# Nine warm-up products instead of fourteen ahead of a two-layer hybrid decoder trunk

## The chip, the cores and the metric
The kernel runs on one core of a Trainium2 chip. The metric is the time of one execution in device microseconds (us), the median of three runs. A NeuronCore has five engines that run side by side and wait for each other by semaphores: PE (TensorE, matrix products), DVE (VectorE), ACT (ScalarE), POOL (GpSimd) and SP (SyncE, which here issues the DMAs). Each engine takes its own instructions strictly in the order in which they stand in the program.

## What is computed
One sequence of 256 tokens with 1024 channels goes through two layers. Each layer normalizes its input, multiplies it by one large input projection, and feeds two groups of heads: attention (8 heads of 128, which for 256 tokens is plain causal attention with a linear distance bias, since no past block exists) and a Mamba-2 state space group (16 heads of 64). Both are gated, joined, and multiplied by an output projection.

```python
def hybrid_layer(x, ln_w, w_in, ...):
    h = rms_norm(x, ln_w)
    proj = h @ w_in
    q, k, v, g_attn, z, xbc, dt_raw = jnp.split(proj, cuts, axis=-1)
    q = rms_norm(q...); k = rms_norm(k...)
    attn = moba_attention(q, k, v) * jax.nn.silu(g_attn)
    xbc = jax.nn.silu(causal_depthwise_conv(xbc, conv_w, conv_b))
    dt = jax.nn.softplus(dt_raw + dt_bias)
    y = ssd_scan(xs, bm, cm, dt, a_log, d_skip) * jax.nn.silu(z)
    y = rms_norm(y, ssd_norm_w)
    return x + jnp.concatenate([attn, y], axis=-1) @ w_out
```

The warm-up products of this study are no part of that: they multiply a tile of ones by itself into a PSUM tile that nobody reads.

## The kernel before
**Weights.** All projections are done in three products, so that float32 accuracy survives a faster product format: with an operand split into a rounded part and a rest, high x high, low x high and high x low are summed in PSUM (lines 226 to 228 for token-major outputs, 244 to 246 for channel-major ones). The weights come in steps of two 128-row slices. Step number i is loaded by SP into `raw` i (line 79), ACT rounds it to `wh` i (line 101), DVE subtracts to get the rest, `wl` i (line 102). There are four `raw` buffers, so the load of `raw` i+4 waits until `wl` i has been computed, and eight pairs of `wh` and `wl`. PE then spends twelve products on a step, the first few of which need only `wh`. Steps 0 to 11 are the value projection v (chunks of 348, 348 and 344 columns), 12 to 27 are q and k, 28 to 39 are the convolved channels x (products `xb`), then the gates g and z, and the output projection.

**The first layer's start.** The transposed input `xT` arrives by DMA and is scaled by the norm's weight without the norm's own factor (`hr`, `lr`, lines 297 and 298), so that the v products can start before the norm is known; the factor is applied to v when it leaves PSUM. Meanwhile ACT sums the squares of the input, POOL takes the power (line 185), DVE puts the factors on a diagonal (`dg`, line 316), PE spreads them over all rows by a product with ones (`rg`, line 321), and DVE multiplies all eight slices of `xT` by them (line 325), which ACT and DVE split into `hT` and `lT` for q, k, x, g and z.

**The warm-up.** Before the first v product, line 165 issues WARM products of a 128 x 128 tile of ones with itself, in plain float32, which the hardware takes as two passes each. They wait for nothing but the memset of the ones (line 159).

**What sets the order.** The kernel is written as a stream of projection steps, between which side work (norms, attention heads, scans) is resumed a given number of steps later (`resume` and `tick`). Yet the order in the program is not that of the source. Except in two regions put under a manual schedule (the first loads and splits on ACT, DVE and SP; the last PE stretch of a layer), the framework orders each engine's instructions by a timeline that it reckons when the kernel is built. What the kernel issues at its start therefore also moves what that timeline puts first later on. Once built, the order is fixed.

**The decay.** From dt_raw, DVE computes a short chain (lines 399 to 412), PE sums it along the sequence (`cp`, line 415), DVE copies it (`cT`, line 418), SP writes it to DRAM (`cd`, line 420) and reads it back twice, broadcast to all 128 partitions, 1 MB each (`cb`, line 423). ACT and DVE make the decay matrices from `cb` (`ehi`, line 470; lines 471 to 474).

**Attention.** After q and k have been normalized (squares `qsq` on ACT, line 342) and transposed (`qtp`, line 354), a head's scores `sp` (lines 362 and 363) are turned into probabilities `sc` by DVE and ACT (lines 365 to 376), transposed by PE (`pp`, line 380) and multiplied by v (`po`, lines 386 and 387).

Of the kernel before, what the change touches and what calls it, by code (L numbers as in the profile page):

```python
# [113 lines left out]


RAWB = 4
WARM = 14
URGENT = 400


# [1 line left out]
def hybrid_kernel(ctx: ExitStack, tc: tile.TileContext, x, par, w, out):  # L122
# [40 lines left out]

    for i in range(WARM):
        pe.matmul(warm[:, 0:P], ones, ones, start=(i == 0), stop=(i == WARM - 1))

# [602 lines left out]
```

## Time and profile before

| | |
|---|---|
| median of three runs | 452.83 us (452.31 to 452.98) |
| the profiled execution's own time | 452.3 us |
| its span, first to last instruction | 450.5 us |
| PE busy | 446.1 us, 99% of the span |
| DVE, ACT, POOL busy | 346.7, 279.7, 23.9 us |
| warm-up products | 28 passes, from 1.05 to 7.02 us |

The span is 1.8 us shorter than the execution's time. A line of the time-ordered view reads: start in us, duration in us, engine, source line, operation, tile written and tiles read, shapes, how many instructions are merged into the line, and in brackets the idle time of the engine ahead of it and what ended it. Matrix products overlap in the pipe, so the distance between two starts, and not the duration, tells what one costs. An engine name that ends in q is its instruction queue; SPq lines are DMA issues. Tile names come without their buffer numbers.

### The profile page before, as it was taken

Reading aid. Unit: us, or ns where it says so; the run is one execution under the profiler, and the core shown is the slowest. Engines: PE = TensorE matmul, PEld = TensorE weight load, DVE = VectorE, ACT = ScalarE, POOL = GpSimd, SP = SyncE. Lnnn points to the kernel's source line nnn. Section 1 sums busy time; section 2 is a strip of 40 time slices with the busy share of each in tenths; the row PEclk is TensorE's granted clock in tenths of the full one; section 3 lists DMA queues with packets and bytes.
Section 4 is the critical chain, followed back from the end, with each engine's and each line's share of the span. In section 5 each row is a group of like instructions: output and inputs, shape, how many; then the busy total and the mean of one; then the engine's idle time right before and its main releaser. Section 6 shows DMA issues by size and latency. Waiting matters only on the chain.

```text
span 450.5 us, 7880 instructions
## 1 busy us (share of the span) xinstructions
PE 446.1 (99%) x2956; PEld 406.0 (90%) x2956; DVE 346.7 (77%) x636; ACT 279.7 (62%) x571; POOL 23.9 (5%) x29
## 2 busy tenths in 40 slices
PE   9999999999999999999999999999999999999997
PEld 9998878999999999888899878889999989998986
DVE  7597876799999888766565784686999999787621
ACT  7776779778558645534556656977657865555400
POOL 0000320200000000000000011110000000000000
PEclk9999999999999999999999999999999999999999
DMA  8888886452355155556246988561435444553301
GB/s 282 275 250 294 284 302 249 143 185 95 95 188 176 60 160 186 169 188 182 61 138 232 284 278 288 185 227 53 139 109 175 139 141 128 200 180 121 121 25 70
DMA packets 26373, 79.43 MB, mean 176 GB/s; under 512 B 2624, under 2 KB 9440, under 8 KB 25824
## 3 DMA queue, kind: packets, MB, share of 16 engines
q1 hardware_dynamic: 26048, 78.68, 53.3%
q8 instruction: 23, 0.38, 0.3%
q10 hardware_dynamic: 288, 0.27, 0.2%
q14 instruction: 14, 0.11, 0.1%
HBM read 77.85 MB, written 1.08 MB: 175 GB/s over the span
## 4 chain that ended last, share of the span: by engine, by line
PE 99%; DVE 0%; issue 0%
PE o L227 6%; PE o L226 6%; PE o L228 6%; PE xb L244 5%; PE xb L246 5%; PE xb L245 5%; PE z L245 3%; PE v L228 3%; PE z L244 3%; PE v L226 3%; PE v L227 3%; PE z L246 3%; PE k L227 3%; PE g L246 3%; PE g L244 3%; PE g L245 3%
## 5 line engine op out<-in xcount | busy, mean ns | idle before, releaser
L102 DVE TENSOR_TENSOR wl<-raw,wh 128x1024 fp32r<-128x1024 f32 (+3 forms) x145 | 166.0, 1157 | 41.3 <-ACT wh L101 40.1
L101 ACT CAST wh<-raw 128x1024 fp32r<-128x1024 f32 (+3 forms) x145 | 143.9, 999 | 59.8 <-DMA raw<-in_w_dram 15.9
L244 PE MATMUL xb<-hT,wh 128*128 128x256 f32 x192 | 56.3, 293 | 0.0
L245 PE MATMUL xb<-lT,wh 128*128 128x256 f32 x192 | 54.4, 283 | 0.0
L246 PE MATMUL xb<-hT,wl 128*128 128x256 f32 x192 | 53.9, 281 | 0.0
L245 PEld LDWEIGHTS xb<-lT,wh 128*128 128x128 f32 x192 | 36.2, 189 | 0.3
L246 PEld LDWEIGHTS xb<-hT,wl 128*128 128x128 f32 x192 | 36.2, 189 | 0.1
L244 PEld LDWEIGHTS xb<-hT,wh 128*128 128x128 f32 x192 | 36.2, 188 | 0.2
L246 PE MATMUL g<-hT,wl 128*128 128x256 f32 x128 | 36.3, 283 | 0.0
L245 PE MATMUL z<-lT,wh 128*128 128x256 f32 x128 | 36.2, 283 | 0.0
L244 PE MATMUL g<-hT,wh 128*128 128x256 f32 x128 | 36.1, 282 | 0.0
L244 PE MATMUL z<-hT,wh 128*128 128x256 f32 x128 | 36.0, 281 | 0.0
L245 PE MATMUL g<-lT,wh 128*128 128x256 f32 x128 | 35.9, 281 | 0.0
L246 PE MATMUL z<-hT,wl 128*128 128x256 f32 x128 | 35.9, 280 | 0.0
L447 DVE SCALAR_TENSOR_TENSOR cv<-rw,par_sb,cv 128x256 f32<-128x256 f32 x72 | 31.6, 481 | 4.2 <-ACT cv L444 4.2
L226 PE MATMUL k<-wh,hT 128*128 128x512 f32 x64 | 25.4, 397 | 0.0
L227 PE MATMUL k<-wh,lT 128*128 128x512 f32 x64 | 25.4, 397 | 0.0
L228 PE MATMUL k<-wl,hT 128*128 128x512 f32 x64 | 25.4, 397 | 0.0
L227 PE MATMUL q<-wh,lT 128*128 128x512 f32 x64 | 25.1, 394 | 0.0
L226 PE MATMUL q<-wh,hT 128*128 128x512 f32 x64 | 25.1, 394 | 0.0
L227 PE MATMUL o<-wh,al 128*128 128x512 f32 (+1 forms) x64 | 24.7, 386 | 0.0
L228 PE MATMUL q<-wl,hT 128*128 128x512 f32 x64 | 24.6, 395 | 0.0
(197 smaller groups left out, 1106.6 us busy)
## 6 DMA issues: line engine op xcount, KB each, us to landing
raw<-in_w_dram SPq DMA_DIRECT2D x120, 512.0 KB, 4.3
raw<-in_w_dram SPq DMA_DIRECT2D x15, 348.0 KB, 3.7
cb<-cd SPq DMA_DIRECT2D x4, 1024.0 KB, 7.8
raw<-in_w_dram SPq DMA_DIRECT2D x8, 344.0 KB, 3.6
x<-in_x_dram SPq DMA_DIRECT2D x2, 512.0 KB, 5.2
xT<-in_w_dram SPq DMA_DIRECT2D x3, 256.0 KB, 4.3
out_dram<-x SPq DMA_DIRECT2D x3, 256.0 KB, 2.0
raw<-in_w_dram SPq DMA_DIRECT2D x2, 174.0 KB, 3.2
```

The costliest lines, as they stand in the source:

```text
L101: nc.scalar.copy(h[:, ks, :wd], src[:, ks, :wd])
L102: nc.vector.tensor_tensor(lo[:, ks, :wd], src[:, ks, :wd], h[:, ks, :wd].bitcast(F32), ALU.subtract)
L226: pe.matmul(ps[:, cs], lh[:, kl, tl], wh[:, kk, cs], start=first, stop=False)
L227: pe.matmul(ps[:, cs], ll[:, kl, tl], wh[:, kk, cs], start=False, stop=False)
L228: pe.matmul(ps[:, cs], lh[:, kl, tl], wl[:, kk, cs], start=False, stop=final)
L244: pe.matmul(o, wh[:, kk, cs], lh[:, k, :], start=(k == 0 and c == 0), stop=False)
L245: pe.matmul(o, wh[:, kk, cs], ll[:, k, :], start=False, stop=False)
L246: pe.matmul(o, wl[:, kk, cs], lh[:, k, :], start=False, stop=(k == KT - 1 and c == 1))
L447: dve.scalar_tensor_tensor(cv[:, c, :], rw[:, c, k:k + S], cw(k), cv[:, c, :], ALU.mult, ALU.add)
```

## The change
The constant WARM goes from 14 to 9. Line 165 then issues nine warm-up products, 18 passes. Nothing else in the source changes.

```diff
 RAWB = 4
-WARM = 14
+WARM = 9
 URGENT = 400
```

The built program changes beyond that, since the framework's ordering comes out otherwise: on PE, DVE, ACT and SP the order differs in the first layer, from step 6 to step 39; all that follows, the whole second layer included, stands in the same order as before.

The first place is on DVE, from the factors of the first norm (`dg0`) on. `wl8` is the low part that v step 8 needs, and the xT rows are the eight multiplications by the spread factors `rg0`. Before:

```order
L316 TENSOR_SCALAR dg0_302<-ident_124,rs0_185 128x128
L102 TENSOR_TENSOR wl7_233<-raw7_212,wh7_232 128x2x348
L102 TENSOR_TENSOR wl8_251<-raw8_218,wh8_250 128x2x344
L325 SCALAR_TENSOR_TENSOR xT_87<-xl_88,rg0_363 128x256
L325 SCALAR_TENSOR_TENSOR xT_87<-xT_87,xl_88,rg0_363 128x256 x5
L102 TENSOR_TENSOR wl9_269<-raw9_224,wh9_268 128x2x344
```

And in the changed program:

```order
L316 TENSOR_SCALAR dg0_297<-ident_119,rs0_180 128x128
L102 TENSOR_TENSOR wl7_228<-raw7_207,wh7_227 128x2x348
L325 SCALAR_TENSOR_TENSOR xT_87<-xl_88,rg0_358 128x256
L325 SCALAR_TENSOR_TENSOR xT_87<-xT_87,xl_88,rg0_358 128x256 x6
L102 TENSOR_TENSOR wl8_246<-raw8_213,wh8_245 128x2x344
L325 SCALAR_TENSOR_TENSOR xT_87<-xT_87,xl_88,rg0_358 128x256
L102 TENSOR_TENSOR wl9_264<-raw9_219,wh9_263 128x2x344
```

Seven multiplications now stand ahead of `wl8`, where there was none.

The second place is on ACT, around the first work on the broadcast `cb`. Before, the rounding of steps 30 and 31 and the squares of q stood ahead of it:

```order
L101 CAST wh30_790<-raw30_734 128x1024
L342 ACTIVATE qsq_818,ss_819<-q10_732 128x128 x4
L355 ACTIVATE qT0_507<-qtp_695,par_sb_86 128x4x128
L355 ACTIVATE qT0_507<-qtp_701,par_sb_86 128x4x128
L101 CAST wh31_846<-raw31_752 128x1024
L342 ACTIVATE qsq_830,ss_831<-q11_733 128x128 x4
L355 ACTIVATE kT0_508<-qtp_806,par_sb_86 128x4x128
L470 ACTIVATE ehi0_0_1318<-cb0_0_203,nac_209 128x128 x4
```

Now they stand behind its first instructions:

```order
L470 ACTIVATE ehi0_0_1313<-cb0_0_198,nac_204 128x128 x4
L470 ACTIVATE ehi1_0_1451<-cb0_0_198,nac_204 128x128 x2
L101 CAST wh30_785<-raw30_729 128x1024
L470 ACTIVATE ehi1_0_1451<-cb0_0_198,nac_204 128x128 x2
L473 ACTIVATE ehi0_0_1313<-ehi0_0_1313 128x512
L342 ACTIVATE qsq_813,ss_814<-q10_727 128x128 x4
L474 ACTIVATE cb0_0_198<-cb0_0_198 128x1024
L342 ACTIVATE qsq_825,ss_826<-q11_728 128x128
L355 ACTIVATE kT0_503<-qtp_801,par_sb_86 128x4x128
L342 ACTIVATE qsq_825,ss_826<-q11_728 128x128 x3
L355 ACTIVATE kT0_503<-qtp_807,par_sb_86 128x4x128
L101 CAST wh31_841<-raw31_747 128x1024
```

Two castings, eight squares and one transposed k have moved behind the wait for `cb` (the other transposed k already stood behind it). On DVE, `cT` has moved ahead of `wl28`, and on SP the write of `cd` and both reads of `cb` have moved ahead of the loads of `raw32` and `raw33`.

The third place is on PE, at the transposition `pp` of the first head's probabilities. Before, it stood two products into step 29:

```order
L246 MATMUL xb5_1072<-hT0_135,wl28_755 128x256
L244 MATMUL xb5_1072<-hT0_135,wh29_772 128x256
L245 MATMUL xb5_1072<-lT0_136,wh29_772 128x256
L380 MATMUL pp_1039<-ident_124,sc_865 128x128
L354 MATMUL qtp_1045<-ident_124,qn_953 128x128
L380 MATMUL pp_1039<-ident_124,sc_865 128x128 x2
```

Now it stands in the middle of step 28, eight products earlier:

```order
L246 MATMUL xb5_1067<-hT0_130,wl28_750 128x256
L380 MATMUL pp_1034<-ident_119,sc_860 128x128
L354 MATMUL qtp_1040<-ident_119,qn_948 128x128 x2
L380 MATMUL pp_1034<-ident_119,sc_860 128x128 x2
L354 MATMUL qtp_1040<-ident_119,qn_948 128x128 x2
L354 MATMUL qtp_1046<-ident_119,qn_960 128x128 x4
L244 MATMUL xb5_1067<-hT0_130,wh28_749 128x256
```

Around it, what was one stretch of attention products in the row of projection products is now two (the scores `sp` that followed `pp` directly come six products later); the same split happens at two other places, so that there are three more such stretches in all. The `cp` product has moved ahead by fourteen products, to step 20.

## Rows read from the trace of the kernel before
**Rows 1.** Page: busy time of PE; the chain that ended last, by engine
```profile
PE 446.1 (99%) x2956; PEld 406.0 (90%) x2956; DVE 346.7 (77%) x636; ACT 279.7 (62%) x571; POOL 23.9 (5%) x29
...
PE 99%; DVE 0%; issue 0%
```
**Rows 2.** PE in order of time, the start (columns as explained above)
```profile
1.05 5.97 PE L165 MATMUL warm<-ones 128*128 128x128 f32 x28 [1.05 <-DVE ones L159]
...
6.53 0.50 PE L165 MATMUL warm<-ones 128*128 128x128 f32 x3
6.78 0.57 PE L226 MATMUL v<-wh,hr 128*128 128x348 f32 x2
...
20.30 0.61 PE L321 MATMUL rg<-dg,ones 128*128 128x128 f32 x4
```
**Rows 3.** Stretches: length, busy per engine, granted clock, DMA share, GB/s
```profile
1.00:1.50 0.50, 0.45 (x2) 0.45 (x3) 0.12 (x4) 0.00 (x0) 0.39 (x1) 1.00 0.00 0
```
**Rows 4.** ACT and DVE in order of time: operands of steps 0 and 1
```profile
4.34 0.46 ACT L101 CAST wh<-raw 128x348 fp32r<-128x348 f32 x1
...
7.41 0.88 DVE L102 TENSOR_TENSOR wl<-raw,wh 128x696 fp32r<-128x696 f32 x1 [0.31 <-ACT wh L101]
```
**Rows 5.** DVE in order of time, dg, wl8, xT and wl9
```profile
19.20 0.29 DVE L316 TENSOR_SCALAR dg<-ident,rs 128x128 f32<-128x128 f32 x1 [0.68 <-POOL rs L185]
...
21.18 0.88 DVE L102 TENSOR_TENSOR wl<-raw,wh 128x688 fp32r<-128x688 f32 x1 [0.73 <-ACT wh L101]
21.97 0.48 DVE L325 SCALAR_TENSOR_TENSOR xT<-xl,rg 128x256 f32<-128x256 f32 x1
...
24.32 0.87 DVE L102 TENSOR_TENSOR wl<-raw,wh 128x688 fp32r<-128x688 f32 x1
```
**Rows 6.** PE in order of time, where steps 8, 9 and 12 need weights
```profile
23.28 0.32 PE L228 MATMUL v<-wl,hr 128*128 128x344 f32 x1
...
24.99 0.32 PE L227 MATMUL v<-wh,lr 128*128 128x344 f32 x1
25.25 0.43 PE L228 MATMUL v<-wl,hr 128*128 128x344 f32 x1
...
29.08 0.62 PE L226 MATMUL q<-wh,hT 128*128 128x512 f32 x2
```
**Rows 7.** SP's issue of raw12, and ACT's rounding of it
```profile
22.09 0.33 SPq L79 DMA_DIRECT2D raw<-in_w_dram  x1
...
26.89 1.05 ACT L101 CAST wh<-raw 128x1024 fp32r<-128x1024 f32 x1 [0.79 <-DMA raw<-in_w_dram]
```
**Rows 8.** PE in order of time: products after a stretch of attention products
```profile
81.02 0.47 PE L244 MATMUL xb<-hT,wh 128*128 128x256 f32 x1
81.32 0.28 PE L245 MATMUL xb<-lT,wh 128*128 128x256 f32 x1
81.44 0.28 PE L246 MATMUL xb<-hT,wl 128*128 128x256 f32 x1
```
**Rows 9.** DVE, SP, ACT and PE in order of time: from cT to pp
```profile
59.64 0.41 DVE L418 COPY cT<-cp 16x256 f32<-16x256 f32 x1
...
64.43 0.80 SPq L423 DMA_DIRECT2D cb<-cd  x2
...
65.97 1.05 ACT L101 CAST wh<-raw 128x1024 fp32r<-128x1024 f32 x1
66.91 0.29 ACT L342 ACTIVATE qsq<-q 128x128 f32<-128x128 f32 x1
...
67.92 0.72 ACT L355 ACTIVATE kT<-qtp,par_sb 128x512 f32<-128x512 f32 x1
68.66 2.46 ACT L470 ACTIVATE ehi<-cb,nac 128x128 f32<-128x128 f32 x8
...
84.03 0.35 DVE L376 TENSOR_SCALAR sc<-sc,ri 128x256 f32<-128x256 f32 x1
...
86.89 0.27 PE L380 MATMUL pp<-ident,sc 128*128 128x128 f32 x1
```

## The prediction
> **What bounds the kernel now.** The page comes first: PE is busy for 446.1 of 450.5 us, and the chain that ended last lies 99% on PE [rows 1]. So the reader is to look at PE alone, ask where it would wait, and take every delay of PE in the first layer as a delay of the end, since behind it no gap is left in which it could be made up. The time-ordered view of PE's start shows 28 warm-up passes from 1.05 us on and the first real product at 6.78 [rows 2]. The operands of that product are there earlier: its weights are rounded at 4.34 + 0.46 = 4.80 us [rows 4]. The warm-up thus holds real work back by nearly 2 us, and this is what the change can win at most.
>
> The next view is DVE's, further on [rows 5]. At 19.49 us the factors of the first norm are done, then come `wl7`, `wl8` and the xT multiplications. Beside it stands PE's view of steps 8 and 9 [rows 6]: the product at 23.28 is the first that needs `wl8`, and the one at 25.25 the first that needs `wl9`. The eleven products from 23.28 to 24.99 take 0.155 us each, and then the twelfth 0.26. This is the one place in the whole trace where PE waits for a split, and the wait is only 0.1 us long, for `wl9` ends at 24.32 + 0.87 = 25.19. PE and DVE are neck and neck at about 25 us; after that, PE's q and k steps are longer than the splits, and PE alone counts.
>
> **The start.** The first 25 passes take 6.53 - 1.05 = 5.48 us, 0.219 each, the last three 0.25 us, 0.083 each [rows 2]. So PE ran at half pace until about 6.5 us, and at full pace from there on. Eighteen passes end at 1.05 + 18 x 0.219 = 5.0 us, and the first product starts there instead of at 6.78. If the pace rises at 6.5 as before, the first 1.5 us of real products go at half pace (0.32 instead of 0.16 us): 4.7 products. The other 7.3 of step 0 take 1.2 us, to 7.7. In step 1 the fifth product needs `wl1`, which ends at 7.41 + 0.88 = 8.29 [rows 4]: a small wait, then eight products to 9.65. Before, step 2 began 24 products and 0.09 us after 6.78, at 10.71. PE is 1.05 us early there.
>
> [...]
>
> **Where the start's gain ends.** At `rg` PE would arrive 1.05 early, at 19.25. But `rg` needs the second `dg`, done at 19.20 + 0.29 = 19.49 [rows 5], which hangs on the landing of the input and not on PE. So `rg` starts at 19.55, and 0.75 us of the lead are left.
>
> **The reordered DVE queue.** `wl7` follows at about 19.55 as before and holds DVE for 0.79 us (21.18 to 21.97 for its like [rows 5]). `rg` takes 0.61 us and is done at 20.16, so the multiplications start at 20.35, right behind `wl7`. Six of them lie between 21.97 and 24.32, 0.392 each; seven take 2.74 us. `wl8`, which was second in the queue, starts at 23.09 and ends at 23.96. PE comes to the product that needs it at 23.28 - 0.75 = 22.53 and waits until 24.02: 0.74 us later than before. The wait at `wl9` (0.10 us) is gone in exchange. Term one: +0.64 us (bounds 0.4 and 0.9). It does not depend on the start at all, since the chain runs from `dg`.
>
> **The load behind wl8.** The load of step 12 waits for `wl8` to free its buffer. It was issued at 22.09, right behind the end of `wl8` at 22.06, and rounded from 26.89 on, 4.80 us later [rows 7]. From 24.0 this makes 28.8, and `wh12` ends at 29.85; PE wants it at 29.08 + 0.64 = 29.72 [rows 6]. Term two: 0.15 us, between 0 (a quicker landing) and 0.5.
>
> **More switches on PE.** After a stretch of plain float32 attention products, the first projection product takes 0.30 us to the next start instead of 0.12 [rows 8]. Three such stretches are added. At 0.18 us each they would cost 0.54, and after mere transpositions, for which these rows give no price, perhaps nothing. Term three: 0.3 us, between 0 and 0.55.
>
> **The probabilities of the first head.** From the start of `ehi` at 68.66, when the broadcast had landed, to the last multiplication of `sc` (84.03 + 0.35) it takes 15.72 us [rows 9], in which ACT is hardly idle. Into this stretch the new order puts two more roundings (65.97 to 66.91: 0.94 each), eight squares (66.91 to 67.92: 1.01 for four) and one transposed k (0.66): 1.88 + 2.02 + 0.66 = 4.56 us. Against that the broadcast comes earlier, since `cT` no longer stands behind `wl28` and its wait: by 1.1 us (the split alone) to 1.9 (with the wait); I take 1.5, for the weights themselves come somewhat later after term two. So `sc` is ready at 84.38 + 4.56 - 1.5 = 87.45. PE reaches `pp` eight products (0.114 each) ahead of the old place and later by terms one, two and a third of three: 86.89 - 0.91 + 0.64 + 0.15 + 0.1 = 86.87. Term four: 0.6 us of waiting, between 0 (a broadcast 2.1 us early) and 1.7 (0.4 early).
>
> Both reads of `cb` now also stand ahead of two loads. [...] The trace shows the two reads issued together at 64.43, with the first one's consumer starting at 68.66 [rows 9]. [...]
>
> Everything behind step 39, and the second layer, is in the old order, and no wait of PE stands there that could swallow a delay. The sum is 0.64 + 0.15 + 0.3 + 0.6 = +1.7 us. On the profiled execution's own 452.3 us (its span of 450.5 and 1.8 around it) it gives 454.0, and on the median of the runs, which is 0.5 higher, 454.5. I predict **454.2 us**.
>
> **Rivals.** *The lead is kept (faster).* If `wl8` ended before PE comes for it, PE would carry its 0.75 us on and be spared the 0.10 at `wl9`: 452.83 - 0.85 = 452.0. It decides at 22.5 us on DVE: the seven multiplications would have to end 1.5 us earlier than by rows 5. Against it stands that `dg` at 19.49 is unmoved and the order is fixed. Chance 0.07.
>
> *Only the early waits count (about the same).* If the broadcast comes 2 us earlier and the added switches are short, terms four and most of three vanish, and +0.6 to +0.9 remain: 453.5. For it speaks that `cT` has moved past a split and a wait; against it that 4.56 us of work have come between. Chance 0.23.
>
> *The wait at pp is the main cost (slower).* If the broadcast is not early at all and the later loads are held up behind it, `sc` comes 2 us later still: 1.1 + 2.6 = +3.7, 456.5. Chance 0.08.
>
> *The pace rises late (slower).* If it rose at 10 us, 3.5 us more would go at half pace, 1.75 us lost, of which 0.3 is covered by the waits at `wl1` and `dg`: `rg` at 21.0 instead of 19.55, its end at 21.6, the chain behind it 1.2 us later (it had 0.2 to spare), and the wait at `pp` gone: 0.64 + 1.2 + 0.15 + 0.3 = +2.3, 455.1. [...] Chance 0.06.
>
> **How the numbers follow.** The forecast, 453.4 to 455.1, has 0.56. A change under 0.2% (0.9 us) is not told from none by a measurement of this kernel. Faster than that: the first rival, 0.07. Within it: the second, and a little of the forecast's lower end, 0.25. Slower: the rest, 0.68. The range of 452.8 to 455.8 leaves out the first rival, the third and a little of the second.
>
> **What would show it.** In the changed profile: the first v product at 5.0 us; `rg` at about 19.55, right after `dg`; seven xT lines ahead of the `wl` of step 8, PE idle for 1.5 us before the product at about 24.0; q's first product at 29.7 to 30.0; PE waiting for `sc` at `pp`, about 87.4. If `wl8` is done by 22.5, or PE does not wait at `pp` and is not behind there, the prediction is wrong in its main steps; if the first v product goes at half pace beyond 8 us, the clock is.

## The result and the profile after

| | before | nine products |
|---|---|---|
| first measurement, median | 452.82 us (452.31 to 453.45, 10 runs) | 456.75 us (453.59 to 458.00, 10 runs) |
| ratio, with its 95% interval | | 1.0073 (1.0049 to 1.0096) |
| second measurement, with the experiments, median | 452.92 us (451.94 to 453.92, 28 runs) | 454.53 us (453.32 to 456.64, 8 runs) |
| ratio, with its 95% interval | | 1.0036 (1.0019 to 1.0053) |
| profiled execution, its span | 452.3, 450.5 us | 457.47, 455.7 us |

The change makes the kernel slower, as forecast, but by 3.9 us in the first measurement, where 1.4 had been forecast, and 456.75 lies above the range. The second measurement, 454.53, lies inside it. Why two measurements of one program differ by 2.2 us (six of ten runs above 456.3 in the first, one of eight in the second) no run shows; it may be chance. New is the spread: 4.7 us over the 18 runs, against about 2 us over the 38 of before. Eleven of the 18 lie below 455, seven above 456.3, none between. In five of the seven the mean granted clock of the run is 0.995 or 0.996; in all others of the 18 it is 0.998 or more.

The page of the profiled execution shows PE no longer alone on the chain that ended last (before: 99% PE [rows 1]):

```profile
PE 446.0 (98%) x2946; PEld 403.6 (89%) x2946; DVE 346.5 (76%) x636; ACT 279.3 (61%) x571; POOL 24.6 (5%) x29
...
PE 79%; DMA 9%; DVE 4%; ACT 3%; issue 2%; SPq 1%; POOL 0%; ACTq 0%; DVEq 0%; POOLq 0%
```

PE is busy as long as before, 446.0 us against 446.1, and now also waits. The view of waits of the same execution names them (what waits, for whom; us in total, times, longest):

```profile
PE pp L380 <- DVE sc L375: 1.9, 1, 1.9
PE v L226 <- ACT wh L101: 1.5, 2, 1.2
PE v L228 <- DVE wl L102: 1.4, 1, 1.4
PE warm L165 <- DVE ones L159: 1.0, 1, 1.0
PE rg L321 <- DVE dg L316: 0.4, 1, 0.4
```

Take them in order of time. PE starts real work at 4.86 us instead of 6.78 [rows 2]:

```profile
1.05 3.73 PE L165 MATMUL warm<-ones 128*128 128x128 f32 x18 [1.05 <-DVE ones L159]
4.86 0.59 PE L226 MATMUL v<-wh,hr 128*128 128x348 f32 x2
5.29 0.48 PE L227 MATMUL v<-wh,lr 128*128 128x348 f32 x2
5.61 0.48 PE L228 MATMUL v<-wl,hr 128*128 128x348 f32 x2
```

In the trace the first fourteen passes start 0.21 us apart and the last four 0.11 us apart: the full pace is there from about 4.2 us on, more than 2 us earlier than in the trace of before (6.5) and after fewer products. PE then waits 0.3 us for the rounded weights. The lead of 1.9 us does not last. In this execution the load of `raw2`, issued at 3.43 us against 3.44 before, lands 2 us late. The rounding of `raw2` on ACT shows it, first before:

```profile
8.16 0.78 ACT L101 CAST wh<-raw 128x696 fp32r<-128x696 f32 x1
```

and after:

```profile
10.13 0.77 ACT L101 CAST wh<-raw 128x696 fp32r<-128x696 f32 x1 [2.07 <-DMA raw<-in_w_dram]
```

The input lands late as well (ACT starts on its second half at 19.07 us, before at 16.99), and `dg` is done at 21.57 us instead of 19.49 [rows 5]. DVE, after:

```profile
21.28 0.29 DVE L316 TENSOR_SCALAR dg<-ident,rs 128x128 f32<-128x128 f32 x1 [0.68 <-POOL rs L185]
21.64 0.88 DVE L102 TENSOR_TENSOR wl<-raw,wh 128x696 fp32r<-128x696 f32 x1
22.45 0.47 DVE L325 SCALAR_TENSOR_TENSOR xT<-xl,rg 128x256 f32<-128x256 f32 x1
22.84 2.43 DVE L325 SCALAR_TENSOR_TENSOR xT<-xT,xl,rg 128x256 f32<-128x256 f32 x6
25.19 0.87 DVE L102 TENSOR_TENSOR wl<-raw,wh 128x688 fp32r<-128x688 f32 x1
```

`wl8` stands behind seven multiplications, and PE waits 1.36 us for it, where before it had none (23.28 [rows 6]):

```profile
24.43 0.32 PE L227 MATMUL v<-wh,lr 128*128 128x344 f32 x1
26.11 0.42 PE L228 MATMUL v<-wl,hr 128*128 128x344 f32 x1 [1.36 <-DVE wl L102]
...
31.80 0.39 PE L226 MATMUL q<-wh,hT 128*128 128x512 f32 x1
```

The first q product is 2.7 us later than the 29.08 of [rows 6]. The other large wait is at the first head's probabilities. On ACT, after:

```profile
70.44 1.87 ACT L470 ACTIVATE ehi<-cb,nac 128x128 f32<-128x128 f32 x6 [4.84 <-DMA cb<-cd]
72.22 1.04 ACT L101 CAST wh<-raw 128x1024 fp32r<-128x1024 f32 x1
```

and on DVE and PE:

```profile
60.95 0.41 DVE L418 COPY cT<-cp 16x256 f32<-16x256 f32 x1
...
90.95 0.35 DVE L376 TENSOR_SCALAR sc<-sc,ri 128x256 f32<-128x256 f32 x1
```
```profile
88.98 0.28 PE L246 MATMUL xb<-hT,wl 128*128 128x256 f32 x1
91.18 0.30 PE L380 MATMUL pp<-ident,sc 128*128 128x128 f32 x1 [1.92 <-DVE sc L375]
```

ACT idles for 4.84 us in front of `ehi`, waiting for the broadcast `cb`, while the castings and squares that filled that time before [rows 9] are queued behind it. `cT` is ahead in DVE's order, yet 1.3 us later than before (60.95 against 59.64), and `ehi` 1.8 us later (70.44 against 68.66). The sum `cp` that `cT` copies is done on PE at 57.81. But two other splits still stand ahead of `cT`, and ACT rounds their weights late, since it has waited for a load. ACT and DVE, after:

```profile
56.58 1.05 ACT L101 CAST wh<-raw 128x1024 fp32r<-128x1024 f32 x1 [1.78 <-DMA raw<-in_w_dram]
```
```profile
57.66 1.23 DVE L102 TENSOR_TENSOR wl<-raw,wh 128x1024 fp32r<-128x1024 f32 x1 [1.25 <-ACT wh L101]
...
59.74 1.23 DVE L102 TENSOR_TENSOR wl<-raw,wh 128x1024 fp32r<-128x1024 f32 x1 [0.76 <-ACT wh L101]
```

### The profile page after: what moved, and what is told of

The parts are those of the page before. It is cut to its first block, busy times and chain, and to the rows that moved or that the text cites. A ratio compares the mean times of both kernels' runs of the same rounds, so it can differ in the third digit from the quotient of the medians.

```text
span 455.7 us, 7859 instructions
## 1 busy us (share of the span) xinstructions
PE 446.0 (98%) x2946; PEld 403.6 (89%) x2946; DVE 346.5 (76%) x636; ACT 279.3 (61%) x571; POOL 24.6 (5%) x29
## 4 chain that ended last, share of the span: by engine, by line
PE 79%; DMA 9%; DVE 4%; ACT 3%; issue 2%; SPq 1%; POOL 0%; ACTq 0%; DVEq 0%; POOLq 0%
DMA raw<-in_w_dram 7%; PE o L227 6%; PE o L226 6%; PE o L228 6%; PE xb L244 4%; PE xb L246 4%; PE xb L245 4%; PE z L245 3%; PE z L244 3%; PE z L246 3%; PE g L246 3%; PE g L245 3%; PE g L244 3%; PE yp L498 3%; ACT wh L101 2%
## 5 line engine op out<-in xcount | busy, mean ns | idle before, releaser
L244 PE MATMUL xb<-hT,wh 128*128 128x256 f32 x192 | 56.2, 293 | 0.0
L245 PE MATMUL xb<-lT,wh 128*128 128x256 f32 x192 | 54.3, 283 | 0.0
L245 PEld LDWEIGHTS xb<-lT,wh 128*128 128x128 f32 x192 | 36.2, 189 | 0.3
L244 PEld LDWEIGHTS xb<-hT,wh 128*128 128x128 f32 x192 | 36.2, 189 | 0.2
L245 PE MATMUL z<-lT,wh 128*128 128x256 f32 x128 | 36.2, 283 | 0.0
L244 PE MATMUL g<-hT,wh 128*128 128x256 f32 x128 | 36.1, 282 | 0.0
L244 PE MATMUL z<-hT,wh 128*128 128x256 f32 x128 | 36.0, 281 | 0.0
L245 PE MATMUL g<-lT,wh 128*128 128x256 f32 x128 | 35.9, 281 | 0.0
L228 PE MATMUL k<-wl,hT 128*128 128x512 f32 x64 | 25.5, 398 | 0.0
L185 POOL TENSOR_TENSOR rr<-se,mhalf 128x4 f32<-128x4 f32 x16 | 18.8, 1178 | 122.2 <-DVE se L344 122.2
L228 PE MATMUL q<-wl,hT 128*128 128x512 f32 x64 | 24.8, 395 | 0.0
```

The costliest lines, as they stand in the source:

```text
L185: pool.tensor_tensor(o, i, mhalf[:, :n], ALU.pow)
L228: pe.matmul(ps[:, cs], lh[:, kl, tl], wl[:, kk, cs], start=False, stop=final)
L244: pe.matmul(o, wh[:, kk, cs], lh[:, k, :], start=(k == 0 and c == 0), stop=False)
L245: pe.matmul(o, wh[:, kk, cs], ll[:, k, :], start=False, stop=False)
```

## The experiments

The framework's order depends on the number of warm-up products, so the change is two changes: a shorter start, and another order. The experiments cross them. The order can be held: an edge that only orders (no semaphore) from each instruction to its neighbour in a list taken from either built program. Every engine then has the wanted order word for word, whatever WARM says.

| kernel | start | order to step 15 | order behind | median, range (us), runs | ratio to before (95%) | runs with clock 0.996 or less |
|---|---|---|---|---|---|---|
| short_start_old_order | 9 | before | before | 453.21, 452.51 to 453.77, 11 | 1.0007 (0.9999 to 1.0016) | 0 |
| long_start_new_order | 14 | after | after | 454.52, 453.49 to 457.62, 9 | 1.0048 (1.0030 to 1.0066) | 1 |
| after_again | 9 | after | after | 454.53, 453.32 to 456.64, 8 | 1.0036 (1.0019 to 1.0053) | 1 |
| short_start_old_early | 9 | before | after | 454.24, 452.73 to 457.44, 12 | 1.0034 (1.0017 to 1.0051) | 1 |
| short_start_old_late | 9 | after | before | 453.57, 453.21 to 454.14, 11 | 1.0009 (1.0001 to 1.0018) | 0 |
| short_start_old_pe | 9 | after, PE before | after, PE before | 454.86, 454.16 to 456.19, 6 | 1.0044 (1.0029 to 1.0059) | 0 |
| short_start_filled_pp | 9 | after | after | 455.90, 455.28 to 456.97, 6 | 1.0068 (1.0054 to 1.0082) | 0 |
| long_start_late_sc | 14 | before | before, ACT loaded | 457.33, 456.68 to 459.03, 5 | 1.0085 (1.0068 to 1.0101) | 2 |
| short_start_x_early | 9 | before, x earlier | before | 452.51, 451.91 to 453.20, 11 | 0.9991 (0.9982 to 1.0000) | 0 |
| short_start_best | 9 | rearranged | before | 451.43, 451.24 to 452.47, 6 | 0.9965 (0.9951 to 0.9980) | 0 |
| short_start_best_again | 9 | rearranged | before | 451.54, 451.21 to 452.46, 11 | 0.9968 (0.9958 to 0.9979) | 0 |
| long_start_best | 14 | rearranged | before | 451.94, 451.09 to 452.55, 7 | 0.9975 (0.9965 to 0.9986) | 0 |

The kernel before, run beside them 78 times in all, had no run with a granted clock under 0.998. Line numbers in the traces of experiments are higher by the lines put in (L244 or L245 is L228, L396 and L402 are L380). What the expectations call raw3 is the load of `raw2`: it was miscounted there.

### Start and order crossed

```diff
-WARM = 14
+WARM = 9
+def hold(tc, nc, shift):
+    made = {i.name: i for b in nc.main_func.blocks for i in b.instructions}
+    for line in ORDER:
+        names = ["I-%d" % (int(n) + shift) for n in line.split()]
+        for a, b in zip(names, names[1:]):
+            tc.add_manual_dep(made[b], a, mybir.DependencyInfo(
+                mybir.DependencyClass.NoSync, mybir.DependencyReason.DATA), reason="order")
...
+    hold(tc, nc, WARM - 14)
```

ORDER holds one row of instruction numbers for each of PE, DVE, ACT and SP. Nine products with the order of before:

> Nine warm-up products, but every engine holds the order that the kernel before has (edges between neighbours fix it); only the start is changed. Order theory (what the prediction went by: the new order costs, the short start does not): 452.0 to 452.9 us, with runs within 1.5 us of each other, PE waiting only at rg for dg (about 0.1 us). Start theory (the two profiles differ first at 8.8 us, where the load of raw3, issued at 3.43 us in both, lands at 10.11 instead of 8.14, and the short warm-up leaves no slack for it): a part of the runs lies at 454 to 455, the input lands near 19.0 instead of 16.9 in those, and the spread of the runs is 2 us or more.

Measured: 453.21, 1.0007 times before, spread 1.3 us. The time is 0.3 us above what the order theory gave, and PE waits for more than `dg`, as the trace below shows; the spread is the order theory's. Then fourteen products with the order of after. WARM stays 14, and ORDER has the other rows; the start of DVE's shows the difference (253 is `wl8`, 366 to 437 are the xT multiplications, 271 is `wl9`):

```diff
-    "235 253 366 367 388 389 414 415 271 436 437 289 ...
+    "235 366 367 388 389 414 415 436 253 437 271 289 ...
```

> Fourteen warm-up products, with the order of the changed kernel on every engine. Order theory: wl8 behind seven xT multiplications and pp eight products earlier cost as in the changed kernel: 454.5 to 457 us. Start theory: raw3 lands at 8.1 us in all runs, so the spread is under 1.5 us as before, and only the waits at wl8 and pp remain: 453.5 to 455.

Measured: 454.52, 1.0048, spread 4.1 us. The median fits both theories, the spread only the order theory. So the short start alone changes nothing that can be told from none, and the new order alone makes both the loss and the spread. The start theory also falls by its trace: in the profiled run of short_start_old_order the input is late too, `dg` ends at 21.06, and the run is still at 453.77. The view of PE and DVE there:

```profile
21.12 0.49 PE L337 MATMUL rg<-dg,ones 128*128 128x128 f32 x2 [0.85 <-DVE dg L332]
...
26.99 0.43 PE L244 MATMUL v<-wl,hr 128*128 128x344 f32 x1 [0.86 <-DVE wl L102]
```
```profile
24.11 2.04 DVE L341 SCALAR_TENSOR_TENSOR xT<-xT,xl,rg 128x256 f32<-128x256 f32 x5
26.07 0.86 DVE L102 TENSOR_TENSOR wl<-raw,wh 128x688 fp32r<-128x688 f32 x1
```

With the old order the lead of the start ends in two waits, 0.85 us at `rg` and 0.86 at `wl9`, which stands behind six multiplications.

The changed kernel once more, on the same chip as these:

> The changed kernel once more, for a second trace of it. Its ten runs so far lie between 453.59 and 458.0, four of them below 454.9 and six above 456.3. If the late raw3 load makes the two groups, a profiled run below 455 shows raw3 landing near 8.1 us and dg near 19.5, one above 456 shows raw3 near 10.1 and dg near 21.3. If the granted clock makes them (0.995 to 0.996 in four of the six long runs), the long runs show a stretch at half pace of 3 to 4 us near the start, whatever raw3 does.

The one long run, 456.64 us, has a clock of 0.996, as four of the first six have, which speaks for the clock as the second alternative has it, though this trace, without a fall, cannot show where the fall lies. The first falls: the profiled run took 454.61 us although its input is late as well (`dg` ends at 20.80). PE waits in it as follows:

```profile
PE v L228 <- DVE wl L102: 1.4, 1, 1.4
...
PE pp L380 <- DVE sc L375: 0.6, 1, 0.6
PE v L226 <- ACT wh L101: 0.5, 1, 0.5
PE rg L321 <- DVE dg L316: 0.3, 1, 0.3
```

The wait at `wl8` is the same 1.4; the one at `pp` is 0.6 instead of 1.9.

### The new order in two pieces

For these, WARM is 9, and each row of ORDER is joined from the two orders at a place where both have had the same instructions (step 15). First the row of before up to there, the new one behind it:

```diff
-    "235 366 367 388 389 414 415 436 253 437 271 289 ...
+    "235 253 366 367 388 389 414 415 271 436 437 289 ...
```

> Nine warm-up products; the order of before up to step 15 on PE, DVE and ACT (wl8 ahead of the xT multiplications again), the new order behind it. By the prediction's terms this takes away term one (0.64) and term two (0.15) and leaves the switches and the wait at pp: 0.9 to 1.5 us under the changed kernel, median 453.0 to 455.5. If instead the wait at wl8 hides behind the late input anyway, or comes back at pp (where sc has its own time), the median is within 0.4 us of the changed kernel's.

Measured: 454.24, 1.0034, with runs up to 457.44. This is 0.3 us under the changed kernel, so the second alternative holds: taking away the first piece hardly helps, and the spread stays. The reverse, new up to step 15 and before behind it:

> Nine warm-up products; the new order up to step 15 (wl8 behind seven xT multiplications), the order of before behind it. If the two pieces of the new order cost separately, this one costs the wait at wl8 alone: 1.4 us of PE's time, less the 0.7 to 1.0 that PE waits anyway for the late input: 453.5 to 454.2 us, no wait at pp, runs within 1.5 us of each other and a granted clock of 0.999 or 1.0 in all. If the spread of the changed kernel comes from the first piece, some runs are above 456.

Measured: 453.57, 1.0009, all runs within 0.9 us. PE waits 1.35 us at `wl8` here, as in the changed kernel, and yet the kernel is level with short_start_old_order (1.0007). Nearly all of the loss, and the spread, therefore sit in the second piece, behind step 15. What the spread is made of, the profiled run of short_start_old_early shows (457.44 us, clock 0.996). PE around `pp`:

```profile
87.56 0.28 PE L262 MATMUL xb<-hT,wl 128*128 128x256 f32 x1
89.76 0.30 PE L396 MATMUL pp<-ident,sc 128*128 128x128 f32 x1 [1.93 <-DVE sc L391]
...
91.68 0.41 PE L260 MATMUL xb<-hT,wh 128*128 128x256 f32 x1
91.89 0.41 PE L261 MATMUL xb<-lT,wh 128*128 128x256 f32 x1
...
94.66 0.28 PE L260 MATMUL xb<-hT,wh 128*128 128x256 f32 x1
94.77 0.28 PE L261 MATMUL xb<-lT,wh 128*128 128x256 f32 x1
```

and the view of stretches (columns as in [rows 3]; the one before DMA share is the granted clock):

```profile
89.80:90.90 1.10, 1.10 (x11) 1.10 (x12) 0.80 (x4) 1.09 (x4) 0.00 (x0) 1.00 0.13 52
91.00:94.30 3.30, 3.30 (x16) 3.12 (x15) 0.94 (x2) 3.03 (x6) 0.00 (x0) 0.50 0.02 5
94.50:97.00 2.50, 2.50 (x22) 2.45 (x21) 2.50 (x7) 1.55 (x4) 0.00 (x0) 1.00 0.01 3
```

PE stands idle for 1.93 us at `pp`, works for 1.1 us at a granted clock of 1.00, and then the granted clock is 0.50 for the 3.3 us of the table's stretch; products start 0.21 us apart instead of 0.11. By that spacing about half of these 3.3 us is lost, an estimate: 1.7 us, besides the 1.9 of the wait.

In this trace 1.93 us of idling stand ahead of the fall; in the first trace of the changed kernel the wait was as long (1.92) and the granted clock stayed at 1.00 (91.1 to 97.0 us), so a fall does not follow every wait of this length.

### PE's order, and PE's idling

ORDER takes PE's row of before and the new rows for DVE, ACT and SP (the only edit against the changed kernel):

> Nine warm-up products; PE in the order of before, DVE, ACT and SP in the new one. pp then stands eight products (0.9 us) later on PE and the three added attention stretches are gone, while sc is as late as in the changed kernel. If the wait at pp is sc's lateness against PE's place, it shrinks by 0.9 us, to 0 to 1.0, and the median is 0.7 to 1.0 us under the changed kernel's, near 453.6, with no run above 456. If the place on PE does not matter, the waits are as before and the median stays at 454.5 or above.

Measured: 454.86, 1.0044, no run above 456.2. The wait at `pp` is gone from the trace (PE comes at 88.88, `sc` is done at 88.56), so the wait is indeed `sc`'s lateness against PE's place. But the median is no better than the changed kernel's, so the first alternative holds for the wait and not for the time. The profiled run (454.87 us) is at the median, and its trace shows where its 2.6 us against the trace of before lie: 1.7 up to the first q product, where PE waits 1.35 us at `wl8` behind a `dg` that is done at 20.56 instead of 19.49; 0.3 from there to the first `xb`; and 0.5 up to the first g product, of which PE waits 0.34 at `bp`. The wait at `pp` is thus not the whole of the loss, and six runs say little about the size of the parts.

Then the wait is filled with work that nobody reads:

```diff
+FILL = 12
...
         pp = bank("pp")
+        for i in range(FILL if h == 0 and not filled else 0):
+            pe.matmul(pp[:, 0:P], ones, ones, start=True, stop=True)
+        filled.append(h)
```

> The changed kernel with its order, and twelve more products of ones by ones (24 passes of 0.083 us, 2.0 us) on PE right ahead of pp of the first head, written into the same PSUM tile before the real transpositions overwrite it. PE then works where it waited. If the long runs of the changed kernel (456.4 and more) come from the clock that falls after the wait at pp (half pace from 90.9 to 94.4 us in the one such trace so far, 1.7 us lost), they vanish: all runs within 454.5 to 456.3, granted clock 0.998 or more in each, although the products themselves cost 0 to 1.4 us. If the clock falls for another reason, some runs still show 0.996 or less and lie above 457.

Measured: 455.90, 455.28 to 456.97, the clock 0.999 or 1.0 in all six. PE in the profiled run:

```profile
88.04 2.84 PE L399 MATMUL pp<-ones 128*128 128x128 f32 x24
90.71 0.27 PE L402 MATMUL pp<-ident,sc 128*128 128x128 f32 x1
```

The passes took 0.11 us each and not 0.083, so they ran 0.5 us past `sc` (done at 90.24), and the two longest runs lie above the expected 456.3. No run shows a fall of the clock. At the changed kernel's rate (5 of 18 runs) one or two of six should have shown it, and none would come about by chance one time in seven; so this speaks for the wait as the cause, but does not prove it.

The other way round, the kernel before is given a late `sc` (start and order of before; twelve copies that nobody reads behind the first `ehi`):

```diff
+LOAD = 12
...
+    junk = const.tile([P, 256], F32, name="junk256")
+    more = [act.activation(junk, base[:, 0:256], AF.Copy).ins.name for _ in range(LOAD)]
+    hold(tc, nc, WARM - 14, more)
```

> The kernel before, its order held, with twelve useless ACT instructions (a copy of 256 columns, some 0.4 us each, 4.8 us in all) behind the first ehi. The probabilities sc of the first head are then as late as in the new order (20.5 us behind the first ehi instead of 15.7), and PE has 2.4 us less than that in hand, so it waits some 2.0 to 2.4 us at pp although start and order are those of before. If a wait of this length at pp lets the clock fall, part of the runs show a granted clock of 0.996 or less and lie 1.5 to 2 us above the rest: 455.0 to 455.8 without the fall, 456.5 to 457.5 with it. If the fall belongs to the new order or to the short start, all runs lie at 455.0 to 455.8 with a clock of 0.999 or more.

Measured: 457.33, 456.68 to 459.03; two of five runs have a clock of 0.996. The two with the lower clock are the 459.03 of the profile and the median, 457.33, which is not above all of the others. The size was missed, because the copies also held up `kT`, which ACT writes behind them, and PE waited for that before it came to `pp`. The profiled run (459.03 us), waits and stretches:

```profile
PE sp L383 <- ACT kT L375: 3.8, 1, 3.8
```
```profile
78.00:82.00 4.00, 0.53 (x3) 0.10 (x1) 2.67 (x8) 4.00 (x11) 0.00 (x0) 1.00 0.00 0
83.10:86.30 3.20, 3.20 (x17) 3.20 (x16) 1.85 (x2) 3.20 (x4) 0.00 (x0) 0.50 0.08 24
86.50:90.00 3.50, 3.50 (x31) 3.45 (x30) 3.49 (x7) 3.50 (x19) 1.27 (x1) 1.00 0.78 283
```

With the start and the order of before, a wait of PE of 3.8 us, for a `kT` that is done at 82.30 (81.63 + 0.67 on ACT), is followed by a granted clock of 0.50 in the stretch from 83.1 us on. So neither the short start nor the new order is needed for the fall. The wait here is twice as long as at `pp`, and so this kernel does not show that 1.9 us are enough; for that stand the trace of short_start_old_early and the counts. Over all kernels in which PE waits at `pp` or at that `sp` (the changed one twice, long_start_new_order, short_start_old_early, long_start_late_sc), 9 of 44 runs have a clock of 0.996 or less; of the 69 runs of the other kernels in the table and the 78 of before, none has.

### A version that beats both

> Nine warm-up products, the order of before, and SP loads x before raw6 instead of behind it, so that dg no longer comes later than PE. If the lead of the short start (1.9 us at the first product) is lost because dg hangs on the input, 0.6 to 1.0 us of it now reach the end: 451.9 to 452.5 us, no wait at rg. If the weights of steps 6 to 8, which now land up to 2.8 us later, or wl1 take it back, the median stays between 452.7 and 453.5.

The two loads of `x` go ahead of `raw6`:

```diff
                 for s in range(KT // KS):
+                    if s == 3:
+                        for t in range(2):
+                            nc.sync.dma_start(x_sb[t], x[t * P:(t + 1) * P, :])
                     ws.pump(s + 1, lambda ks: first_tokens(
...
-                for t in range(2):
-                    nc.sync.dma_start(x_sb[t], x[t * P:(t + 1) * P, :])
                 nc.sync.dma_start(par_sb, par)
```

Measured: 452.51, 0.9991. `rg` no longer waits, but `wh6` now stands behind the squares of x on ACT, and PE waits 0.74 us for it at 18.25. So only the first half of `x` goes ahead of `raw6`, `wh6` is rounded between the squares of the two halves, and DVE's row becomes, by names,

```
dg, wl7, xT, xT, wl8, xT, wl9, xT x5, wl10, ...
```

```diff
+                    if s == 3:
+                        nc.sync.dma_start(x_sb[0], x[0:P, :])
                     ws.pump(s + 1, lambda ks: first_tokens(
...
-                for t in range(2):
-                    nc.sync.dma_start(x_sb[t], x[t * P:(t + 1) * P, :])
+                nc.sync.dma_start(x_sb[1], x[P:2 * P, :])
```

> Nine warm-up products, PE and SP in the order of before but for one load: the first half of x is loaded before raw6, the second right behind it. ACT rounds wh6 between the squares of the two halves, and DVE does two xT multiplications, wl8, one more, wl9, and then the others. If the lead of the start is lost to the input, to wh6 behind the squares and to wl9 behind six multiplications, 0.9 to 1.2 us of it reach the end: 451.5 to 452.2 us, PE ahead of the kernel before by about 1.0 us up to the q products. If the landings of raw7 and raw8 bind instead, it is no better than with both halves early, 452.2 to 452.9.

Measured: 451.43, 0.9965. DVE and PE of its profiled run:

```profile
21.15 0.87 DVE L102 TENSOR_TENSOR wl<-raw,wh 128x688 fp32r<-128x688 f32 x1
21.94 0.47 DVE L341 SCALAR_TENSOR_TENSOR xT<-xT,xl,rg 128x256 f32<-128x256 f32 x1
22.33 0.87 DVE L102 TENSOR_TENSOR wl<-raw,wh 128x688 fp32r<-128x688 f32 x1
```
```profile
19.72 0.61 PE L337 MATMUL rg<-dg,ones 128*128 128x128 f32 x4
...
28.32 0.63 PE L242 MATMUL q<-wh,hT 128*128 128x512 f32 x2
```

`wl8` and `wl9` end at 22.02 and 23.20, before PE wants them, and the first q product is 0.76 us ahead of the 29.08 of [rows 6]. Is it the start or the rearrangement? The next kernel has WARM = 14 and is otherwise the same; the nine products run once more beside it.

> As short_start_best, with fourteen warm-up products instead of nine, the same order on every engine. If the gain of short_start_best (0.35% under before) is the lead of the short start, now kept, this one is no faster than before: 452.6 to 453.2 us. If it is the earlier input and the new places of wl8 and wl9 alone, it lies at 451.4 to 451.9 as well.

> The same kernel as short_start_best once more, for more runs beside those with fourteen products on one chip: 451.2 to 452.5 us again, under long_start_best by 0.5 to 1.2 us if the start makes the gain, equal to it within 0.3 us if the order makes it.

Measured side by side: 451.94 (0.9975) with fourteen products, 451.54 (0.9968) with nine. It is mostly the rearrangement: it gives 1.2 us. The five products give 0.4 more, which overlapping intervals do not tell from none.

## Why the prediction was wrong

The times of PE's milestones in the profiled runs show where each one's loss lies. Behind the first g product all take 327 us, the kernel before too: as the prediction said, no delay is made up there. The first two columns are times from the span's start, the others lengths, all in us.

| profiled run | `dg` done | first q product | from there to the first `xb` | from there to the first g product |
|---|---|---|---|---|
| before | 19.49 | 29.08 | 49.97 | 44.29 |
| changed, first measurement | 21.57 | 31.80 | 50.40 | 46.30 |
| after_again | 20.80 | 31.07 | 49.82 | 44.96 |
| long_start_new_order | 20.17 | 30.44 | 49.80 | 45.25 |
| short_start_old_early | 20.24 | 30.30 | 50.48 | 48.00 |
| short_start_old_late | 20.09 | 30.35 | 49.98 | 44.29 |
| short_start_old_pe | 20.56 | 30.82 | 50.26 | 44.82 |
| short_start_old_order | 21.06 | 30.84 | 49.98 | 44.29 |

**The start** came near what was worked out, but not in the way it was: the first product stands at 4.86 (5.0 predicted), with the full pace from 4.2 us and not from 6.5, and then a wait for `wh`. The 0.083 us taken for a pass at full pace is a misreading; passes start 0.11 us apart, and only from the last of them to the first real product it is 0.03. The lead is used up at `wh`, `wl` and `dg`. In long_start_best 28 passes took 5.18 us instead of the 5.97 of [rows 2], so this time varies by itself. The late-rise rival (at 10 us) does not occur in any trace whose start was read: with nine warm-up products the v products stand 0.16 us apart from 5.29 us on in the changed kernel but for its waits, and from 5.64 and 5.62 in the two traces of short_start_best. That the rise depends on the number of warm-up products no run shows.

**The first step that failed** is the premise of term one, said with the first rival, that *"`dg` at 19.49 is unmoved"*. It was read from one trace of before, an execution of 452.3 us, at the lower end of its ten runs (452.31 to 453.45). In the other nine traces that load x behind `raw6`, `dg` is done between 20.1 and 21.6 us, at 20.2 and 20.4 in the two that have the long start. In the profiled run of the first measurement this is 2.1 of the 3.5 us by which the span exceeds the one predicted (455.7 against 452.2).

**Term one** (0.64 us for `wl8`) had the chain from `dg` right: it put the first q product at 29.72, 10.23 us behind `dg`, and in all six traces with seven multiplications ahead of `wl8` it is 10.2 to 10.3 us behind `dg`. The wait, 1.36 us, was near the 1.49 worked out. But what it replaces was taken as the 0.10 us at `wl9` of [rows 6]; with a short start and the old order that wait is 0.86, and `rg` waits as well. By the medians of short_start_old_late and short_start_old_order (1.0009 and 1.0007) the net price is 0.1 us, with about 0.4 us of uncertainty on either.

**Term two** (0.15 us, the load behind `wl8`) was near zero: no wait for `wh12` stands in the traces.

**Term three** (0.3 us for the switches) was near zero too. In after_again and long_start_new_order the stretch with `pp` is 0.67 and 0.96 us longer than before, of which 0.59 and 0.87 are the wait at `pp`, and the stretch ahead of it is 0.15 and 0.17 us shorter.

**Term four** (0.6 us) is the second step that failed, at *"I take 1.5"* for the earlier broadcast. ACT's stretch from `ehi` to the end of `sc` is 91.30 - 70.44 = 20.86 us, near the 15.72 + 4.56 = 20.28 worked out. But `ehi` did not start 1.5 us earlier than 68.66. It started between 1.2 us earlier and 1.8 us later, at 70.44, 67.81, 67.44 and 69.03 in the four traces with the new order and PE waiting at `pp` (changed kernel twice, long_start_new_order, short_start_old_early), because `cT` is earlier in the order only: it still stands behind splits that wait for their weights, in the first trace for a late load, and it starts 1.6 to 3.7 us after `cp` is done. The write of `cd` and the read of `cb` vary besides: from the issue of the write to that of the first read 4.30 us pass before and 4.03 after, and the reads land 4.1 and 7.7 us after their issue before, 4.9 and 8.3 after. The wait at `pp` was 1.9, 0.6, 0.9 and 1.9 us instead of 0.6. The old order does not care: in short_start_old_order `ehi` starts at 72.22, later than in any of these, and `pp` goes without a wait at 88.66, since ACT did the other work while the broadcast was under way.

**What no rival had** is the granted clock behind a wait: 0.50 for 3.3 us in the trace of short_start_old_early, about 1.7 us more. Four of the first ten runs have a clock of 0.995 or 0.996; without 1.7 us in each of them the median would be 455.6 by this estimate, just inside the range. The third rival (456.5 us, chance 0.08: broadcast not early, `pp` the main cost) describes the first measurement best, though in four of its six long runs the last 1.7 us would by the same estimate be the clock's. That the second measurement lies near the forecast is in part luck: in its trace 2.0 us are lost up to q, where 0.64 had been reckoned, and 0.5 behind it, where 1.05 had been.

**Open** stays why the early loads land up to 2 us later in some executions. The landings vary with either start (`dg`, which waits for the input, is done at 19.49 and 20.17 us in the table's two rows with the long one, at 20.09 to 21.57 in the six with the short one), and that the short start has a part in it is not ruled out. Two of the long runs of the changed kernel (456.37, 457.47) need no fall of the clock. The first has no trace; for the other, late input (2.7 us up to q) and the full wait at `pp` (1.9) make up 4.6 of the 5.2 us by which its span is longer.

## What to carry to other kernels

Where a framework orders the instructions by its own reckoning, a constant changed at the start is two changes, and one holds the order by edges to see either alone. A new wait on the bound engine is priced with what was measured behind such waits (here a granted clock of 0.50 for some 3.3 us in two traces, and a clock of 0.996 or less in 9 of 44 runs), and the landing of an input or a broadcast, read from one trace, is taken as a range and not as a point (here `dg` at 19.49 to 21.57 us, `ehi` at 67.44 to 70.44). For the broadcast, the work queued behind its consumer decided whether its lateness cost anything (`ehi` at 72.22 with no wait at `pp`, at 70.44 with 1.92 us). An early start is worth only as much as each later supplier (input, splits) is early too: of 1.9 us at the first product nothing was left at the first q product, which was 2.7 us late.

## What the runs showed of the hardware

After PE had waited 1.93 us in short_start_old_early and 3.8 us in long_start_late_sc, the granted clock was 0.50 in stretches of 3.3 and 3.2 us. In the first case it began 1.1 us after work had been resumed, in the second 0.8 us or less after `kT`, for which PE waited, was done. After another wait of 1.92 us, in the first trace of the changed kernel, it stayed at 1.00. The full pace at the start came at different times, not ordered by the number of warm-up products. With nine it was there at about 4.2 us in one execution (18 passes in 3.73 us) and by 5.64 in another (18 passes in 4.21 us, short_start_best). With fourteen it came at 6.5 [rows 2], and in long_start_best, where 28 passes took 5.18 us instead of 5.97, at about 4.9, an estimate from these 0.79 us and the two distances between passes, 0.21 and 0.11. A 348 KB load issued at the same time (3.43 and 3.44 us) had its consumer start at 8.16 in one execution and 10.13 in another.
